# A constant tile of the decoder-trunk kernel declared 24 columns wide, 16 of them used

## The chip, the core and the metric

One core of a Trainium2 chip runs the whole kernel. The metric is the device time of one execution in microseconds (us). The profile is of one execution of the same program; its span runs from the first to the last instruction. The engines are TensorE (PE, with its weight loads listed apart as PEld), VectorE (DVE), ScalarE (ACT), GpSimd (POOL) and the DMA queues, most of them issued from SyncE (SP).

## What is computed

One layer of a hybrid decoder trunk on x of 512 positions by 2048 features, all in float32:

```
h = rms_norm(x, norm1_w)
proj = h @ w_in                       # 2048 x 5648: q, k, v | z, xBC | dt
attn = moba_attention(rms_norm(q), rms_norm(k), v)      # 8 heads of 128, causal blocks of 256
xbc  = silu(causal_dwconv(xBC))       # width 4
dt   = softplus(dt_raw + dt_bias);  a = -exp(a_log)     # 16 heads
y    = ssd_chunked_scan(xs, dt, a, bm, cm) + d_skip * xs
ssm  = rms_norm(y * silu(z))
x = x + concat(attn, ssm) @ w_out     # 2048 x 2048
u = causal_dwconv(rms_norm(x) @ w_up) # 2048 x 11264, width 3
return x + (silu(u_gate) * u_val) @ w_down              # 5632 x 2048
```

The tile that is changed holds exp(a_log), once per partition: 16 float32 values, one per head.

## The kernel before

**Splitting.** Every large product is made of fp32r matmuls. An operand v is split into `hi` = v rounded to fp32r (ACT, lines 1428 and the like) and `lo` = v - hi (DVE, line 1437 and the like), and a product is hi.hi + hi.lo + lo.hi: three matmuls for each pair of 128x128 stationary and 128xN moving tile. Each matmul loads its own stationary tile (LDWEIGHTS) before it streams the moving one. In the profile's names, `x<-cmb,hi` is output, then moving tile, then stationary tile.

**Stages, in order of time.**
1. To 78 us: z and the first quarter of v. The x tiles A (hi) and B (lo), 16 of each, are stationary; the split weights `hi2`/`lo2` move (names `s<-hi,A`, `y<-hi,A`, 512 and 256 columns).
2. 78 to 298 us: q, k of five heads and x, B, C, by 2x2 block products of which only seven are computed instead of eight (P1 to P7), for 11 groups of column blocks. A product is 24 matmuls of 256 columns: `hi2`/`lo2` are stationary. P1, P2 and P3 move A and B; P4, P5, P6 and P7 move the tile TK, which holds sums and differences of blocks of x.
3. 298 to 753 us: the rest of the projection (names `acc<-hi,A` and `acc<-A,hi`), attention (tiles `qh`, `ql`, `kh`, `kl`, `PTh`, `PTl`, `vh`, `vl`), the scan, and the projection w_out with A, B moving in 512 columns.
4. 753 to 2095 us: the main part. 44 groups for w_up, then 24 for w_down (three passes over 7, 8 and 7 blocks), each again seven products; the moving operand is one of the seven tiles cmb0 to cmb6 (hi and lo halves of eight 256-column blocks), the stationary one `hi2`/`lo2`. A w_up product is 24 matmuls (8 x 3), a w_down product 21 or 24. In code, with h, l the split weights and bk the cmb tile:

```
for q in part:
    w = h[:, q * 128:(q + 1) * 128]
    pe.matmul(out, w, bk[:, 0, q, :], ...)          # line 1693
    pe.matmul(out, w, bk[:, 1, q, :], ...)          # line 1694
for q in part:
    pe.matmul(out, l[:, q * 128:(q + 1) * 128], bk[:, 0, q, :], ...)   # line 1696
```

Around each product k of stage 4 a list written out by hand sets the order: the product's output is taken from PSUM (lines 1540 to 1568), then sums of weight blocks for later products (lines 1409 to 1417 on DVE, 1402 on POOL), the `lo` of product k+2 (`split_lo`, line 1437), the convolution and gating work (lines 1578 to 1603), and the `hi` of product k+3 (`split`, line 1428). Weight blocks are loaded six to eight products ahead into `rawa` and `rawb`. There are three `hi2` buffers and two `lo2` buffers.

**Where tiles lie.** On-chip memory is given out from two ends. Pools on the left grow upwards from a low address, in the order in which they are opened, pools on the right downwards from the top, and every tile's row is rounded up to a multiple of 32 bytes. `ea_log` (line 301) is the last tile of the pool `consts`, the first pool on the left. Behind it on the left come `ring` (rawa, hi2, lo2), `ab` (A, B; later `w2`: par2, rawb, acc_s) and `rb` (rawb of stage 2). On the right lie TK, all cmb tiles, the attention and scan tiles and the work tiles of the later stages. Several tiles are used from a column offset on: hi2 and lo2 from column 20, 36 or 52 (`W_OFF`, lines 1427, 1436, 1097, 1104), A and B from 36 (`X_OFF`), TK from 20, cmb from 4 (`F_OFF`).

First byte used, counted along a partition, in the program before (slices within a tile begin multiples of 64 bytes later):

| tile | side | address of first byte used | remainder by 64 | by 256 |
|---|---|---|---|---|
| hi2 / lo2, stages 1 and 3 | left | 23424 / 36480, + 80, buffers 4352 apart | 16 | 208 |
| hi2 / lo2, stage 2 | left | same, + 208 | 16 | 80 |
| hi2 / lo2, stage 4 | left | same, + 144 | 16 | 16 |
| A0..A15, B0..B15 | left | 45184 and 82048, + 144, 2304 apart | 16 | 16 |
| TK | right | 155360 + 80 | 48 | 48 |
| cmb0 to cmb4 / cmb5 / cmb6 | right | 146144, 16640 apart / 112864 / 129504, each + 16 | 48 | 240 |
| PTh, PTl | right | 120640 and 124736, + 512 | 0 | 64 |
| vh, vl | right | 172640, 176736 or 221152, 225248 | 32 | 96 or 224 |
| kl, ql | right | 158144 and 152000, buffers 2048 apart | 0 | 192 |
| qh | right | 164288, buffers 2048 apart | 0 | 192 |
| kh | right | 168544, buffers 2048 apart | 32 | 96 |

ea_log itself is written by one ACT exponential (line 436) and read by one DVE instruction (line 448), both over 16 columns.

Of the kernel before, what the change touches and what calls it, by code (L numbers as in the profile page):

```python
# [20 lines left out]
F32 = mybir.dt.float32  # L21
# [186 lines left out]
def body(ctx, tc, xT, wi, wz, wq, wv1, wv, wz1, wo, wu, wd0, wd1, wd2, pp, pf, outT, dbg={}):  # L208
# [6 lines left out]
    consts = ctx.enter_context(tc.tile_pool(name="consts", bufs=1))  # L215
# [82 lines left out]
    rstd = consts.tile([128, 4], F32, name="rstd")  # L298
    epsms = consts.tile([128, 4], F32, name="epsms")
    nhalf = consts.tile([128, 8], F32, name="nhalf")  # L300
    ea_log = consts.tile([128, 16], F32, name="ea_log")

    def pc(name, i=0, n=1):
        o = _PC[name] + i
# [1426 lines left out]
```

## Time and profile before

| | |
|---|---|
| median of 3 runs | 2097.41 us (2097.01 to 2098.18) |
| the profiled execution | 2097.41 us; its span 2095.7 us |
| mean granted TensorE clock | 0.999 |
| PE busy | 2079.4 us, 99% of the span |
| PEld busy | 2004.7 us, 96% |
| DVE busy | 1646.0 us, 79% |
| ACT busy | 1033.1 us, 49% |
| POOL busy | 229.3 us, 11% |
| DMA | 349.77 MB, 167 GB/s on average |
| stage 4 | 753 to 2095 us |

A matmul's row shows from start to modelled end some 0.28 us for 256 columns, but matmuls are pipelined: what counts is the distance from one start to the next, which is what "pace" means below. It is found by dividing a stretch of time by the number of matmuls that start in it.

### The profile page before, as it was taken

How to read it: one execution, taken by the hardware profiler on the slowest of the kernel's cores; microseconds unless marked ns; L12 is line 12 of the kernel's file. 1: busy time of each engine (PE TensorE's matmuls, PEld its weight loads, DVE VectorE, ACT ScalarE, POOL GpSimd, SP SyncE). 2: the span in 40 equal slices, each digit the busy share in tenths (PEclk: the TensorE clock that was granted, in tenths of full speed). 3: DMA queues.
4: the chain of work that ended last, by engine and by line, in shares of the span. 5: the costliest groups of instructions: out<-in, count | busy, mean ns of one | idle time of the engine just before them, and what ended most of it. 6: DMA issues, size and time to landing. Idle time of an engine off the chain costs nothing.

```text
span 2095.7 us, 39004 instructions
## 1 busy us (share of the span) xinstructions
PE 2079.4 (99%) x15958; PEld 2004.7 (96%) x15958; DVE 1646.0 (79%) x2209; ACT 1033.1 (49%) x1467; POOL 229.3 (11%) x137
## 2 busy tenths in 40 slices
PE   9999999999999999999999999999999999999999
PEld 8999998898888899999999999999999999999998
DVE  7787856656655479889898988988989987866876
ACT  7545444554444345454454544545445645544532
POOL 0011100000100001101011010110101111111110
PEclk9999999999999999999999999999999999999999
DMA  5544443343445454444444544544446668657753
GB/s 173 181 151 153 170 159 127 131 151 126 136 141 181 160 185 160 146 159 156 156 162 142 181 151 142 178 143 163 154 159 220 214 178 244 215 161 230 233 193 112
DMA packets 125778, 349.77 MB, mean 167 GB/s; under 512 B 12000, under 2 KB 36512, under 8 KB 122784
## 3 DMA queue, kind: packets, MB, share of 16 engines
q1 hardware_dynamic: 123296, 338.90, 47.4%
q0 software_dynamic: 2304, 8.39, 2.4%
q8 instruction: 125, 2.05, 0.4%
q14 instruction: 53, 0.43, 0.1%
HBM read 293.20 MB, written 54.03 MB: 166 GB/s over the span
## 4 chain that ended last, share of the span: by engine, by line
PE 97%; DVE 2%; ACT 1%; issue 0%; DMA 0%; SPq 0%; ACTq 0%; DVEq 0%
PE x L1694 18%; PE x L1693 18%; PE x L1696 18%; PE acc L203 16%; PE x L203 9%; PE sm L203 4%; PE y L1694 3%; PE y L1696 3%; PE y L1693 3%; PE y L203 3%; PE s L203 2%; DVE lo L1437 0%; DVE cmb L1488 0%; DMA rawa<-wz 0%; ACT hi L203 0%
## 5 line engine op out<-in xcount | busy, mean ns | idle before, releaser
L1693 PE MATMUL x<-cmb,hi 128*128 128x256 f32 x3152 | 773.6, 282 | 3.6 <-ACT hi L1428 1.9
L1694 PE MATMUL x<-cmb,hi 128*128 128x256 f32 x3152 | 773.8, 283 | 0.0
L1693 PEld LDWEIGHTS x<-cmb,hi 128*128 128x128 f32 x3152 | 592.8, 188 | 5.1 <-issue 3.9
L1694 PEld LDWEIGHTS x<-cmb,hi 128*128 128x128 f32 x3152 | 596.0, 189 | 0.0
L1696 PE MATMUL x<-cmb,lo 128*128 128x256 f32 x3152 | 444.4, 283 | 0.7 <-DVE lo L1437 0.6
L1696 PEld LDWEIGHTS x<-cmb,lo 128*128 128x128 f32 x3152 | 406.4, 189 | 1.4 <-DVE lo L1437 1.4
L1428 ACT ACTIVATE hi<-s 128x1024 fp32r<-128x1024 f32 (+1 forms) x203 | 202.5, 998 | 244.3 <-DVE s L1409 125.8
L1437 DVE TENSOR_TENSOR lo<-s,hi 128x1024 fp32r<-128x1024 f32 (+1 forms) x203 | 241.0, 1187 | 38.8 <-issue 36.2
L1402 POOL TENSOR_TENSOR rawb<-rawa,rawb 128x1024 f32<-128x1024 f32 (+1 forms) x66 | 161.2, 2443 | 928.2 <-DVE s L1409 907.9
L1437 DVE TENSOR_TENSOR lo<-rawa,hi 128x1024 fp32r<-128x1024 f32 (+1 forms) x206 | 244.4, 1186 | 19.7 <-PE x L1696 15.8
L1428 ACT ACTIVATE hi<-rawa 128x1024 fp32r<-128x1024 f32 (+1 forms) x206 | 211.4, 1027 | 16.0 <-PE x L1694 15.5
L203 DVE TENSOR_TENSOR lo<-rawa,hi 128x1024 fp32r<-128x1024 f32 (+3 forms) x119 | 136.0, 1143 | 68.5 <-PE acc L203 36.2
L1560 ACT ACTIVATE cP<-x 128x256 f32<-128x256 f32 x131 | 50.5, 386 | 238.8 <-PE x L1696 238.8
L203 ACT ACTIVATE hi<-rawa 128x1024 fp32r<-128x1024 f32 (+3 forms) x120 | 118.6, 989 | 93.7 <-PE acc L203 71.2
L203 PE MATMUL acc<-A,hi 128*128 128x512 f32 x352 | 139.6, 397 | 0.0
L203 PE MATMUL acc<-A,lo 128*128 128x512 f32 x352 | 136.8, 389 | 0.0
L203 PE MATMUL acc<-B,hi 128*128 128x512 f32 x352 | 136.7, 388 | 0.0
L1694 PE MATMUL y<-cmb,hi 128*128 128x256 f32 x544 | 133.6, 283 | 0.0
L1693 PE MATMUL y<-cmb,hi 128*128 128x256 f32 x544 | 133.4, 282 | 0.0
L1437 DVE TENSOR_TENSOR lo<-rawb,hi 128x1024 fp32r<-128x1024 f32 (+1 forms) x67 | 79.9, 1192 | 39.5 <-PE x L1696 38.2
L1694 PEld LDWEIGHTS y<-cmb,hi 128*128 128x128 f32 x544 | 102.8, 189 | 0.0
L1693 PEld LDWEIGHTS y<-cmb,hi 128*128 128x128 f32 x544 | 102.3, 188 | 0.0
(277 smaller groups left out, 3428.1 us busy)
## 6 DMA issues: line engine op xcount, KB each, us to landing
rawa<-wu SPq DMA_DIRECT2D x176, 512.0 KB, 3.7
rawa<-wd SPq DMA_DIRECT2D x64, 448.0 KB, 4.1
rawa<-wi SPq DMA_DIRECT2D x44, 512.0 KB, 3.9
gd<-gt SPq DMA_DIRECT2D x22, 1024.0 KB, 4.2
rawb<-wu SPq DMA_DIRECT2D x43, 512.0 KB, 4.6
rawa<-wo SPq DMA_DIRECT2D x32, 512.0 KB, 3.7
rawa<-wd SPq DMA_DIRECT2D x32, 512.0 KB, 4.0
ld<-gd SPq DMA_DIRECT2D x27, 512.0 KB, 7.3
```

The costliest lines, as they stand in the source:

```text
L203: return fn(out, *args, **kw)
L1402: (po if gi != 1 else ve).tensor_tensor(r, raw[gi, "11"][:, :n], r, op=OP.subtract)
L1428: se.activation(h[:, :n], src[:, :n], AF.Copy)
L1437: ve.tensor_tensor(l[:, :n], src[:, :n], h[:, :n].bitcast(F32), op=OP.subtract)
L1560: se.activation(g[x], X[:, 256:512] if x == "P5" else X[:, :256], AF.Copy)
L1693: pe.matmul(out, w, bk[:, 0, q, :], start=fresh and q == 0, stop=False, skip_group_check=True)
L1694: pe.matmul(out, w, bk[:, 1, q, :], start=False, stop=False, skip_group_check=True)
L1696: pe.matmul(out, l[:, q * 128:(q + 1) * 128], bk[:, 0, q, :], start=False, stop=q == n - 1, skip_group_check=True)
```

## The change

The tile is declared with 24 columns and cut back to its first 16. Its rounded row grows from 64 to 96 bytes, so the pools behind it on the left (ring, ab, rb, w2) begin 32 bytes later. Tiles of consts, and all tiles on the right, stay where they are. No instruction, size, wait or order is edited.

```
-    ea_log = consts.tile([128, 16], F32, name="ea_log")
+    ea_log = consts.tile([128, 24], F32, name="ea_log")[:, :16]
```

## The prediction, made before the changed kernel was run

> **What bounds the kernel.** I read the page's totals and its chain of waits first, then the costliest groups, then busy times by stage, and then starts of single matmuls.
>
> ```profile
> span 2095.7 us, 39004 instructions
> PE 2079.4 (99%) x15958; PEld 2004.7 (96%) x15958; DVE 1646.0 (79%) x2209; ACT 1033.1 (49%) x1467; POOL 229.3 (11%) x137
> ...
> PE 97%; DVE 2%; ACT 1%; issue 0%; DMA 0%; SPq 0%; ACTq 0%; DVEq 0%
> PE x L1694 18%; PE x L1693 18%; PE x L1696 18%; PE acc L203 16%; PE x L203 9%; PE sm L203 4%; PE y L1694 3%; PE y L1696 3%; PE y L1693 3%; PE y L203 3%; PE s L203 2%; DVE lo L1437 0%; DVE cmb L1488 0%; DMA rawa<-wz 0%; ACT hi L203 0%
> ```
>
> TensorE carries 97% of the chain and hardly ever waits. So the time is the number of matmuls times their pace, and only a change of pace can move it much. The pace in the main part, w_up and w_down, comes from a table by stretches (columns: length, busy time and instructions of each engine, granted clock, DMA share, GB/s) and from the counts of the groups.
>
> ```profile
> 753.00:1641.00 888.00, 887.05 (x7394) 886.85 (x7393) 799.92 (x990) 452.28 (x587) 107.88 (x44) 1.00 0.47 162
> 1641.00:2095.00 454.00, 447.69 (x3710) 445.45 (x3708) 346.05 (x401) 212.42 (x271) 69.52 (x39) 1.00 0.64 200
> ...
> 1000.00:1403.20 403.20, 403.20 (x3362) 403.20 (x3361) 362.47 (x450) 201.25 (x260) 49.14 (x20) 1.00 0.45 157
> ```
> ```profile
> L1693 PE MATMUL x<-cmb,hi 128*128 128x256 f32 x3152 | 773.6, 282 | 3.6 <-ACT hi L1428 1.9
> L1693 PE MATMUL y<-cmb,hi 128*128 128x256 f32 x544 | 133.4, 282 | 0.0
> ```
>
> In 403.20 us 3360 matmuls start (3362 touch the stretch, two of them begun before it): a pace of 120.0 ns at full granted clock. Lines 1693, 1694 and 1696 each have 3152 + 544 = 3696 of them, 11,088 in all, and 11,088 x 120.0 ns = 1330.6 us is nearly all of stage 4.
>
> The row that decides the prediction is in stage 2, where the same three-matmul pattern with 256 columns runs with two kinds of moving tile. Rows of the order of time (start, length, what):
>
> ```profile
> 157.72 0.28 PE L203 MATMUL x<-A,hi 128*128 128x256 f32 x1
> ...
> 159.53 1.07 PE L203 MATMUL x<-A,lo 128*128 128x256 f32 x8
> 160.44 2.08 PE L203 MATMUL x<-TK,hi 128*128 128x256 f32 x16
> 162.35 1.12 PE L203 MATMUL x<-TK,lo 128*128 128x256 f32 x8
> 163.31 0.88 PE L203 MATMUL x<-TK,hi 128*128 128x256 f32 x6
> ```
>
> A product that moves A and B takes 160.44 - 157.72 = 2.72 us for 24 matmuls, a pace of 113.3 ns. The next, which moves TK, takes 163.31 - 160.44 = 2.87 us, a pace of 119.6. Stationary buffers, columns, clock and code are the same. By the table of addresses, A and B lie at 16 past a multiple of 64 bytes, as the stationary hi2 and lo2 do, and TK lies at 48. The cmb tiles of stage 4 also lie at 48 against stationary tiles at 16, and run at TK's pace.
>
> Two more pairs separate readings of this. In attention, PTh and PTl (remainder 0) move against vh and vl (remainder 32), and kl (0) moves against qh (0), with ql (0) loaded next.
>
> ```profile
> 609.98 0.28 PE L203 MATMUL sm<-PTh,vh 128*128 128x256 f32 x1
> ...
> 611.39 0.40 PE L203 MATMUL acc<-A,hi 128*128 128x512 f32 x1
> ```
> ```profile
> L203 PE MATMUL acc<-A,lo 128*128 128x512 f32 x352 | 136.8, 389 | 0.0
> ...
> L203 PE MATMUL sm<-kh,ql 128*128 128x512 f32 x8 | 3.2, 396 | 0.0
> L203 PE MATMUL sm<-kl,qh 128*128 128x512 f32 x8 | 3.1, 389 | 0.0
> ```
>
> The 12 matmuls of PTh and PTl take 611.39 - 609.98 = 1.41 us, a pace of 117.5: slow, although the moving tile begins on a multiple of 64. In 512 columns, kl against qh takes 389 ns from start to end, as A against lo2 does (16 against 16), and kh against ql (32 against 0) 396; that last pair is weak evidence, since another kind of matmul follows it. So neither remainder of the moving tile alone explains the pace. What fits all rows is the difference of the two: no difference modulo 64 is fast (16/16, 0/0), a difference of 32 slow (48/16, 0/32, 32/0). By 256 the fast differences are 0, 64 and 192, the slow ones 96, 160 and 224, moving minus stationary. That the two streams, a matmul's moving tile and the next one's weights, get in each other's way in memory is my reading, not something a row names.
>
> **The change, part by part.** No instruction is added or taken away; ea_log's writer and reader keep address and size, so that part costs nothing, and needs no cover. All else is the shift of the left side by 32 bytes.
>
> *Stage 4.* Stationary hi2/lo2 go from 16 to 48, the cmb tiles stay at 48: difference 0 modulo 64, and 240 - 48 = 192 modulo 256, exactly that of A against hi2 in stage 2 (16 - 80), which ran at 113.3. So 11,088 x (120.0 - 113.3) ns = 74 us less. Bounds: nothing gained at one end; the other end is that row's 113.3, the fastest pace of any 256-column product shown.
>
> *Stage 2.* The products that move TK become 48/48, difference 192 modulo 256 too.
>
> ```profile
> L203 PE MATMUL x<-TK,hi 128*128 128x256 f32 x688 | 89.6, 283 | 1.0 <-DVE u L203 0.6 <-ACT cP L203 0.4
> ...
> L203 PE MATMUL x<-TK,lo 128*128 128x256 f32 x344 | 48.2, 282 | 0.0
> ...
> L203 PE MATMUL y<-TK,hi 128*128 128x256 f32 x16 | 2.1, 282 | 0.0
> ...
> L203 PE MATMUL y<-TK,lo 128*128 128x256 f32 x8 | 1.1, 282 | 0.0
> ```
>
> 688 + 344 + 16 + 8 = 1056 matmuls x (119.6 - 113.3) ns = 7 us less.
>
> *Left against left* (A, B with hi2, lo2, in stages 1 to 3) shifts together and keeps its differences; attention and scan lie on the right and do not move: nothing, between zero and the cost in the second rival.
>
> *Who is late next.* With 168 matmuls of a w_up group at 113.3 ns, PE needs 19.04 us instead of 20.16. DVE is the next engine:
>
> ```profile
> 1378.12:1398.28 20.16, 20.16 (x170) 20.16 (x169) 18.15 (x25) 10.06 (x14) 2.45 (x1) 1.00 0.41 138
> ...
> 1620.16:1640.32 20.16, 20.16 (x170) 20.16 (x169) 19.51 (x23) 14.32 (x19) 2.72 (x1) 1.00 0.44 137
> 1640.32:1660.48 20.16, 19.64 (x162) 19.25 (x161) 20.16 (x24) 14.15 (x19) 2.72 (x1) 1.00 0.74 252
> ...
> 1781.44:1801.60 20.16, 20.07 (x167) 19.90 (x167) 20.16 (x21) 14.57 (x19) 3.82 (x2) 1.00 0.92 296
> ...
> 1942.72:1962.88 20.16, 19.98 (x166) 19.77 (x166) 20.16 (x25) 13.46 (x17) 3.60 (x2) 1.00 0.88 279
> ```
>
> DVE's 362.47 us in the twenty groups from 1000 to 1403.20 are 18.1 us a group, 0.9 below PE's new need, so w_up stays bound by PE. At the three changes of pass, where the splits of the cmb tiles (line 1488) come on top, DVE is already busy all of 20.16 us, and PE cannot run ahead of it: each such stretch keeps its length over one to two groups, 1.1 to 2.2 us not gained, 3 to 7 us together; I take 5. ACT (10.06 of 20.16) and the DMA (share 0.45) have room for loads that come 6% more often.
>
> Sum: 74 + 7 - 5 = 76 us less than 2097.4, which is both the profiled execution's own time (span 2095.7 and 1.7 around it) and the median of the three runs: **2021 us**.
>
> **Rivals.** *No change.* The pace could hang on something that differs between A and TK other than the low bits: A and B step 2304 bytes from one block to the next, TK and cmb 1024. Against it: the stationary tiles step 512 bytes, so the two streams meet at many multiples of 256 apart, and within stage 2 every A product is fast and every TK product slow; and cmb5 (from 112864) overlies addresses of B14 and B15, which are fast in stage 2. For it: no row shows cmb, or any right-hand moving tile of 1024-byte steps, going fast. The time would then be 2097.4. The Trainium skill, page "TensorE: Matmul & The Clock Gate", section "Step-by-step: what each phase is for", says TensorE has two independent read ports and that "Loading the next tile's weights doesn't steal SBUF read bandwidth from the running matmul." By that rule the relative address cannot matter, and the change would give the same 2097.4; the A and TK rows (113.3 against 119.6) speak against it, unless the cause lies elsewhere.
>
> *Slower.* The slow case could be "either tile begins in the upper half of 64 bytes": 48/16, 0/32 and 32/0 fit that as well, and no row shows a pair with both in the upper half. Then stage 4 stays at 120, and what is fast now, at 16/16, turns slow at 48/48.
>
> ```profile
> L203 PE MATMUL acc<-A,hi 128*128 128x512 f32 x352 | 139.6, 397 | 0.0
> ...
> L203 PE MATMUL x<-A,hi 128*128 128x256 f32 x168 | 39.5, 277 | 0.6 <-DVE v L203 0.6
> ...
> L203 PE MATMUL acc<-hi,A 128*128 128x256 f32 x128 | 37.7, 295 | 0.0
> ...
> L203 PE MATMUL acc<-hi,A 128*128 128x512 f32 x64 | 26.2, 410 | 0.0
> ...
> L203 PE MATMUL s<-hi,A 128*128 128x512 f32 x64 | 25.2, 394 | 0.0
> ...
> L203 PE MATMUL y<-A,hi 128*128 128x256 f32 x96 | 22.7, 278 | 0.0
> ...
> L203 PE MATMUL acc<-hi,A 128*128 128x272 f32 x64 | 19.3, 302 | 0.5 <-ACT v L203 0.5
> ...
> L203 PE MATMUL y<-hi,A 128*128 128x256 f32 x64 | 18.1, 282 | 2.6 <-ACT hi L203 2.6
> ```
>
> By three matmuls each (hi.hi, hi.lo, lo.hi) that is 3 x (352 + 64 + 64) = 1440 of 512 columns and 3 x (168 + 128 + 96 + 64 + 64) = 1560 of 256 or 272. At 6.3 ns each for the narrow ones, and for the wide ones from 6.3 (if the cost is one for a matmul) to 12.6 (if it goes by columns), 19 to 28 us more: 2116 to 2125. It decides if A's products in stage 2 go from 2.72 to 2.87 us. Two streams meeting gives no reason for a fixed half, so I hold it less likely.
>
> *DVE takes the bound.* If DVE's 2.0 us of idle time a group (20.16 - 18.1) did not shrink, because its waits for PE and ACT in order cost the same, w_up would gain nothing: stage 4's gain falls to the 24 w_down groups, 3696 x 6.7 ns = 25 us, and with stage 2's 7 and the 5 lost at the pass changes 27 us less, 2070. Half of it gives about 2046. Against it: most of that idle time is waiting for PE itself, and `lo` of a product is issued two products ahead.
>
> **How the numbers follow.** Difference modulo 64, gain nearly whole (2010 to 2045): 0.76. DVE takes half or more (2045 to 2075): 0.08. No change: 0.09. Slower: 0.07. A measurement of this kernel tells about 0.2%, 4 us, from no change; so faster 0.84, same 0.09, slower 0.07. The range runs from 2008, where neither pass changes nor waits take anything back, with the rounding of the paces, to 2060, which takes in most of the third rival and leaves out no change and slower.
>
> **What would show it.** Right: in stage 4 a w_up product's 24 matmuls in 2.72 us instead of 2.88, TK's products likewise, A's unchanged, a group in about 19.0 us, DVE busy over 94% of w_up. Wrong: stage 4 still at 120 ns (rival one), A's products at 2.87 (rival two), or 113 ns within products with waits of PE for `lo` (line 1437) between them (rival three).

## The result, and the profile after

The changed kernel takes 2024.24 us (median of 4 runs, 2024.06 to 2024.38), against 2097.21 us for the kernel before beside it: a ratio of 0.9652, 95% interval 0.9635 to 0.9668, 73.0 us less. The profiled execution took 2024.33 us. Totals and chain of waits of the page after:

```profile
span 2022.6 us, 39004 instructions
...
PE 2002.2 (99%) x15958; PEld 1925.6 (95%) x15958; DVE 1640.7 (81%) x2209; ACT 1034.6 (51%) x1467; POOL 231.0 (11%) x137
...
PE 93%; DVE 4%; DMA 1%; issue 1%; ACT 1%; SPq 0%; DVEq 0%; ACTq 0%
```

The instruction counts are those of before, one for one. PE's busy time falls by 77 us and DVE's by 5: the same matmuls went faster. Busy times by stretches (w_up, w_down, then twenty w_up groups):

```profile
748.00:1589.50 841.50, 839.53 (x7398) 838.67 (x7397) 797.62 (x990) 454.85 (x589) 108.94 (x44) 1.00 0.50 172
1589.50:2022.60 433.10, 423.87 (x3693) 420.37 (x3691) 342.95 (x400) 210.62 (x269) 69.88 (x39) 1.00 0.67 208
...
1000.00:1380.80 380.80, 380.80 (x3363) 380.80 (x3362) 361.36 (x451) 201.68 (x260) 49.63 (x20) 1.00 0.48 167
```

The 3360 matmuls that start in the last stretch now take 380.80 us instead of 403.20: 113.3 ns each instead of 120.0, at the same granted clock of 1.00. In stage 2 (order of time; start, length, what):

```profile
155.32 0.28 PE L203 MATMUL x<-A,hi 128*128 128x256 f32 x1
...
157.13 1.07 PE L203 MATMUL x<-A,lo 128*128 128x256 f32 x8
158.04 1.98 PE L203 MATMUL x<-TK,hi 128*128 128x256 f32 x16
159.85 1.07 PE L203 MATMUL x<-TK,lo 128*128 128x256 f32 x8
160.76 1.98 PE L203 MATMUL x<-TK,hi 128*128 128x256 f32 x16
```

The product that moves A still takes 158.04 - 155.32 = 2.72 us. TK's takes 160.76 - 158.04 = 2.72 too, where it took 2.87.

How much came from where: the first row of each fence below is the first matmul of stage 4, the second the last seven of its last product, before and then after.

```profile
752.85 0.28 PE L1693 MATMUL x<-cmb,hi 128*128 128x256 f32 x1
...
2091.03 1.00 PE L1696 MATMUL x<-cmb,lo 128*128 128x256 f32 x7
```
```profile
746.48 0.28 PE L1693 MATMUL x<-cmb,hi 128*128 128x256 f32 x1
...
2018.01 0.95 PE L1696 MATMUL x<-cmb,lo 128*128 128x256 f32 x7
```

Stage 4 begins 6.4 us earlier, nearly all of it from stage 2 (the matmul that began at 73.9 us begins 0.3 earlier, the one at 314.2 us 6.5 earlier), and gains 73.0 - 6.4 = 66.6 us itself. Its 11,088 matmuls at 113.33 instead of 120.0 ns would give 73.9, so 7.3 were given back. The chain of waits after shows where (start, length, what it went through):

```profile
751.60 2.48 DMA xd<-gx
754.10 6.07 DMA ld<-xd
760.19 1.07 ACT cmb L1522
762.43 1.06 DVE s L1417
763.72 1.14 DVE lo L1437
764.90 1.21 PE x L1696 x8
1569.78 1.13 DVE lo L1437
...
1584.22 1.09 PE x L1696 x7
```

And DVE at the three changes of pass (by stretches, columns as above):

```profile
1584.80:1604.00 19.20, 18.04 (x152) 17.30 (x151) 19.20 (x23) 13.68 (x19) 2.71 (x1) 1.00 0.77 256
1730.00:1745.00 15.00, 13.82 (x117) 13.26 (x116) 15.00 (x16) 10.75 (x13) 4.15 (x2) 1.00 0.86 273
1884.00:1898.00 14.00, 12.87 (x107) 12.13 (x106) 14.00 (x18) 8.24 (x11) 3.59 (x2) 1.00 0.88 265
```

DVE is busy all the time there and PE has gaps of 1.1 to 1.2 us in each. Added up over all distances between starts in stage 4, what lies above the pace is 15.7 us after and 8.5 before. Of the 7.2 more, 5.5 lie at the three changes of pass (2.5, 1.5 and 1.5) and 1.0 in the first 25 us of stage 4, counting only distances more than 60 ns above the pace; smaller distances make up the remaining 0.8. In those 25 us the chain goes through transfers of `xd` and `ld`, which do not get shorter: by the pages' medians 2.6 and 5.9 us before, 2.5 and 6.6 after.

### The profile page after: what moved, and what is told of

Its sections match the earlier page's. It is cut to its first block, busy times and chain, and to the rows that moved or that the text cites. A ratio compares the mean times of both kernels' runs of the same rounds, so it can differ in the third digit from the quotient of the medians.

```text
span 2022.6 us, 39004 instructions
## 1 busy us (share of the span) xinstructions
PE 2002.2 (99%) x15958; PEld 1925.6 (95%) x15958; DVE 1640.7 (81%) x2209; ACT 1034.6 (51%) x1467; POOL 231.0 (11%) x137
## 4 chain that ended last, share of the span: by engine, by line
PE 93%; DVE 4%; DMA 1%; issue 1%; ACT 1%; SPq 0%; DVEq 0%; ACTq 0%
PE acc L203 17%; PE x L1696 17%; PE x L1693 17%; PE x L1694 17%; PE x L203 8%; PE sm L203 5%; PE y L1693 3%; PE y L1694 3%; PE y L1696 3%; PE y L203 3%; PE s L203 2%; DVE lo L1437 1%; DVE cmb L1488 1%; DVE lo L203 0%; DVE s L1417 0%
## 5 line engine op out<-in xcount | busy, mean ns | idle before, releaser
L1693 PE MATMUL x<-cmb,hi 128*128 128x256 f32 x3152 | 736.4, 276 | 6.0 <-ACT hi L1428 3.0
L1694 PE MATMUL x<-cmb,hi 128*128 128x256 f32 x3152 | 734.6, 275 | 0.0
L1696 PE MATMUL x<-cmb,lo 128*128 128x256 f32 x3152 | 424.1, 275 | 1.6 <-DVE lo L1437 1.4
L1696 PEld LDWEIGHTS x<-cmb,lo 128*128 128x128 f32 x3152 | 387.7, 188 | 2.8 <-DVE lo L1437 2.8
L1694 PE MATMUL y<-cmb,hi 128*128 128x256 f32 x544 | 126.7, 275 | 0.0
L1693 PE MATMUL y<-cmb,hi 128*128 128x256 f32 x544 | 126.7, 275 | 0.0
```

The source lines that it names most:

```text
L1693: pe.matmul(out, w, bk[:, 0, q, :], start=fresh and q == 0, stop=False, skip_group_check=True)
L1694: pe.matmul(out, w, bk[:, 1, q, :], start=False, stop=False, skip_group_check=True)
```

## The experiments

Below, "difference" is the first byte of the moving tile minus that of the stationary one, modulo 256, in stage 4. It was 224 in the kernel before and is 192 in the changed one. The theory of the prediction was that the difference modulo 64 sets the pace; the rivals here are a place of the weights alone, or of some other tile on the left. All kernels keep every instruction of before unless it is said.

**Reach the same difference another way.** Three edits to the kernel before, by column offsets (4 bytes a column): the weights of stage 4 alone by 32 bytes; the cmb tiles alone by 32; the change and the cmb tiles together, back to difference 224.

```
e1  before, lines 1427, 1436:  hi_tile(36), lo_tile(36)  ->  hi_tile(44), lo_tile(44)     # 192
e2  before, line 36:           F_OFF = 4  ->  12                                          # 0
e3  changed kernel, line 36:   F_OFF = 4  ->  12                                          # 224
```

> ea_log as before, 16 wide; only the split weights of stage 4 begin 32 bytes later in their tiles, so hi2/lo2 lie at 48 against cmb at 48. Difference theory (the pace hangs on the address of the moving tile minus that of the weights, modulo 64): stage 4 at 113.3 ns, TK's products still at 119.6, so 2024 + 7 = 2031 us. Weights' place (stationary tiles are faster at 48 than at 16, wherever the moving ones lie): 2031 as well. Other left tiles (rawa, rawb, A, B, acc_s or the DMA into them gained from the shift): 2097.

> ea_log 16 wide, weights at 16 as before; the cmb tiles are used from column 12 instead of 4, so they lie at 16 (48 + 32 modulo 64). Difference theory: stage 4 at 113.3, 2031 us. Weights' place: weights unmoved, 2097. Other left tiles: 2097.

> ea_log 24 wide as in the change, and cmb from column 12: weights at 48, cmb at 16, difference 32 again. Difference theory: stage 4 back at 120 ns, only stage 2 gains, 2097 - 7 = 2090 us. Weights' place and other left tiles: both as after the change, 2024.

Measured: e1 2029.77 us (ratio 0.9678, 0.9662 to 0.9694), e2 2081.08 (0.992, 0.9905 to 0.9935), e3 2091.13 (0.997, 0.996 to 0.9981). Twenty w_up groups, 3360 starts, in e1, e2 and e3 in turn:

```profile
1000.00:1380.80 380.80, 380.80 (x3363) 380.80 (x3362) 361.34 (x451) 201.91 (x260) 49.44 (x20) 1.00 0.48 167
```
```profile
1000.00:1397.60 397.60, 397.60 (x3363) 397.60 (x3362) 362.43 (x451) 201.58 (x261) 49.26 (x20) 1.00 0.46 159
```
```profile
1000.00:1403.20 403.20, 403.20 (x3363) 403.20 (x3362) 362.50 (x451) 201.42 (x260) 49.12 (x20) 1.00 0.45 157
```

The paces are 113.3, 118.3 and 120.0 ns. e1 shows that the weights of stage 4 are all that matters of the left side there, and leaves 2029.77 - 2024.24 = 5.5 us for stage 2. e3 has every left tile where the change puts it, and is slow again: neither the weights' place alone nor another left tile is the cause, the places of weights and moving tile together are. But e2 refutes modulo 64: there the two begin on the same remainder by 64, and the pace is 118.3.

**How far does it go?** ea_log declared 32 columns wide (left side 64 bytes later than before), and then, from the changed kernel, other columns for the weights of stage 4.

```
e4     before, line 301:               [128, 16]  ->  [128, 32] cut to [:, :16]    # 160
m64    changed, lines 1427 and 1436:   column 36  ->  4                            # 64
m128                                   36  ->  52                                  # 128
m176                                   36  ->  40                                  # 176
m208                                   36  ->  32                                  # 208
m32                                    36  ->  12                                  # 32
m96                                    36  ->  60                                  # 96
```

> ea_log declared 32 wide: the left side shifts by 64 bytes instead of 32. Difference theory, period 64: every difference modulo 64 as before, 2097 us. If the period is 128 or 256 the differences are new (cmb minus weights 160 instead of 224 modulo 256) and the time may be anything between 2024 and 2097. Other left tiles: some of the gain stays, well below 2097.

> The changed kernel with the weights of stage 4 taken from column 4 instead of 36, 128 bytes earlier: moving minus stationary goes from 192 to 64 modulo 256, nothing else. So far (256-column pace in stage 4): 0: 118.3, 160: 116.7, 192: 113.3, 224: 120.0 ns. Period 128: 64 is the same as 192, 113.3 ns, 2024 us. Period 256: 64 is a place of its own, anything from 109 to 120 ns, 2024 - 48 = 1976 to 2024 + 74 = 2098 us; another pace than 113.3 refutes period 128.

> The changed kernel with the weights of stage 4 taken from column 52: difference 128 modulo 256. Period 128: as difference 0 (118.3 ns), 2024 + 11088 x 5.0 ns = 2079 us. Period 256: another pace. If the cost were a matter of how far apart the two streams are within the period, a half period from 0 would be the fastest, at or below 113.3 ns, 2024 us or less.

> The changed kernel with the weights of stage 4 taken from column 40: difference 176 modulo 256, 16 bytes from the fast 192 towards the 160 that ran at 116.7 ns. If the cost goes by pieces of 32 bytes, 176 is as 160 (116.7 ns, 2024 + 11088 x 3.4 ns = 2062 us) or as 192 (113.3 ns, 2024 us). If it goes smoothly with the difference, half way: 115.0 ns, 2043 us.

> The changed kernel with the weights of stage 4 taken from column 32: difference 208 modulo 256, 16 bytes from the fast 192 towards the slow 224. By pieces of 32 bytes: as 192 (113.3 ns, 2024 us) or as 224 (120.0 ns, 2024 + 74 = 2098 us). Smoothly: half way, 116.7 ns, 2061 us.

> The changed kernel with the weights of stage 4 taken from column 12: difference 32 modulo 256. The multiples of 32 tried so far gave 0: 118.3, 64: 118.3, 128: 120.0, 160: 116.7, 192: 113.3, 224: 120.0 ns. If only a narrow place near 192 is fast: 116.7 to 120 ns, 2024 + 11088 x (3.4 to 6.7) ns = 2062 to 2098 us. If every second or third place were as fast as 192 and the change did not need just this one: 113.3 ns, 2024 us.

> The changed kernel with the weights of stage 4 taken from column 60: difference 96 modulo 256, the last multiple of 32 not tried. Narrow place near 192: 116.7 to 120 ns, 2062 to 2098 us. Otherwise 113.3 ns, 2024 us.

The same twenty groups in e4, m64, m128, m176, m208, m32 and m96 in turn:

```profile
1000.00:1392.00 392.00, 392.00 (x3362) 392.00 (x3361) 362.44 (x451) 201.67 (x261) 49.33 (x21) 1.00 0.47 162
```
```profile
1000.00:1397.60 397.60, 397.60 (x3362) 397.60 (x3361) 362.32 (x452) 201.63 (x260) 49.36 (x20) 1.00 0.45 160
```
```profile
1000.00:1403.20 403.20, 403.20 (x3362) 403.20 (x3361) 362.50 (x450) 201.39 (x261) 49.12 (x20) 1.00 0.45 157
```
```profile
1000.00:1400.80 400.80, 400.80 (x3363) 400.80 (x3362) 362.41 (x451) 201.41 (x260) 49.22 (x20) 1.00 0.45 158
```
```profile
1000.00:1400.40 400.40, 400.40 (x3362) 400.40 (x3361) 362.37 (x451) 201.36 (x260) 49.13 (x20) 1.00 0.45 158
...
1830.00:1900.00 70.00, 70.00 (x603) 70.00 (x602) 45.29 (x45) 30.29 (x40) 10.70 (x7) 1.00 0.66 196
```
```profile
1000.00:1397.60 397.60, 397.60 (x3363) 397.60 (x3362) 362.52 (x451) 201.46 (x261) 49.18 (x21) 1.00 0.45 160
```
```profile
1000.00:1403.20 403.20, 403.20 (x3362) 403.20 (x3361) 362.51 (x450) 201.29 (x260) 49.12 (x20) 1.00 0.45 157
```

| difference | kernel | pace, ns | time, us |
|---|---|---|---|
| 0 | e2 | 118.3 | 2081.08 |
| 32 | m32 | 118.3 | 2075.07 |
| 64 | m64 | 118.3 | 2074.16 |
| 96 | m96 | 120.0 | 2091.47 |
| 128 | m128 | 120.0 | 2092.07 |
| 160 | e4 | 116.7 | 2062.05 |
| 176 | m176 | 119.3 | 2084.17 |
| 192 | changed kernel; e1 | 113.3 | 2024.24; 2029.77 |
| 208 | m208 | 119.2 | 2081.71 |
| 224 | before; e3 | 120.0 | 2097.21; 2091.13 |

(e1 and e2 lack stage 2's gain, as before does.) Of ten places, eight of them all the multiples of 32, only 192 is fast; 16 bytes to either side it is 119. A period of 64 is out (0 and 128 against 192), and so is one of 128 (64 against 192). The seven cmb tiles lie on both remainders by 512, and within w_up the products of all seven have the same pace in each kernel (to 0.1 ns), so 256 is enough as a period. That the difference alone sets the pace was tried with more than one pair of places at 192 and 224 only: 192 is 113.3 with cmb at 240 against weights at 48, A at 16 against 80, and TK at 48 against 112 (all modulo 256); 224 is 119.6 to 120.0 with cmb at 240 against 16, cmb at 16 against 48, and TK at 48 against 80. Every other row of the table stands for one pair of places. Neither smoothness nor steps of 32 bytes held: 176 is slower than both its neighbours. In m208 the pace also depends on more than the difference, since the last quoted row of it, in the pass with eight blocks, has 600 starts in 70.00 us, 116.7 ns, against 119.2 in w_up. No formula for the pace came out of this map.

**Which weights does a moving tile meet: its own, or the next one's?** The kernel before with only `lo2` moved to difference 192 (line 1436), `hi2` left at 224; and the kernel before with half as many stationary columns in lines 1694 and 1696.

```
lo_only  line 1436:  lo_tile(36)  ->  lo_tile(44)
half_w   line 1694:  pe.matmul(out, w, ...)        ->  pe.matmul(out[:64, :], w[:, :64], ...)
         line 1696:  pe.matmul(out, l[.. 128], ..) ->  pe.matmul(out[:64, :], l[.. 64], ..)
```

> The kernel before (ea_log 16 columns) with only lo2 of stage 4 taken 32 bytes later: hi2 stays at difference 224 from cmb, lo2 goes to 192. If each matmul's pace goes with its own pair or with the weights loaded beside it, the third of the matmuls that uses lo2 runs at 113.3 and the rest at 120: mean 117.8 ns, 2097.7 - 3696 x 6.7 ns = 2073 us, and starts in a run of lo2 matmuls 113 to 114 ns apart. If the pace is one rhythm of the whole stream, set by its slower part, 120 throughout: 2098 us.

> The kernel before, with 64 instead of 128 stationary columns in the matmuls of lines 1694 and 1696, so hi.lo and lo.hi are added to the first 64 output partitions only; the number of matmuls, their 256 moving columns and all addresses stay (difference 224). Two streams meeting: the 16 of 24 matmuls beside which a half load runs lose much of the 6.7 ns: pace 113.3 to 117, 2097.7 - 11088 x (3 to 6.7) ns = 2023 to 2064 us. If the load of the weights has no part in it and the moving stream alone is slow: 120 ns, 2098 us.

Measured: lo_only 2074.91 us (0.9888, 0.9872 to 0.9904), half_w 2075.92 (0.9895, 0.9879 to 0.9911). Both have 3360 starts in 395.80 us, 117.8 ns:

```profile
1000.00:1395.80 395.80, 395.80 (x3363) 395.80 (x3362) 362.43 (x451) 201.46 (x261) 49.25 (x20) 1.00 0.46 160
```
```profile
1000.00:1395.80 395.80, 395.80 (x3362) 395.80 (x3362) 362.44 (x451) 201.18 (x260) 49.31 (x20) 1.00 0.46 160
```

Starts in lo_only, in order of time:

```profile
1001.42 1.07 PE L1696 MATMUL y<-cmb,lo 128*128 128x256 f32 x8
1002.33 0.28 PE L1693 MATMUL x<-cmb,hi 128*128 128x256 f32 x1
...
1004.25 1.07 PE L1696 MATMUL x<-cmb,lo 128*128 128x256 f32 x8
```

The eight `lo` matmuls take 1002.33 - 1001.42 = 0.91 us, some 114 ns each; the sixteen `hi` ones 1.92 us, 120.0 each. So the pace belongs to single matmuls, not to one rhythm of the stream, and the price is as expected. The ends of these runs tell which. Over the products after 800 us, a `lo` matmul followed by `lo` is followed after 113 ns (median). The last `lo`, beside which the next `hi2` is loaded, is followed after 117; the last `hi`, beside which `lo2` is loaded, after 114. In the kernel before both are 124, in the changed one 114 and 113. (Within a slow product the distances are not equal: in the kernel before their medians go 118, 117, 122, 124 over and over, so 117 is one of the slow ones, and 120 is their mean.) A matmul's own stationary tile would give the opposite. What counts is the moving tile and the weights loaded while it moves. That agrees with the reading in the prediction. It speaks against the rule of the Trainium skill cited there, page "TensorE: Matmul & The Clock Gate", section "Step-by-step: what each phase is for", that loading the next tile's weights takes no SBUF read bandwidth from the running matmul: here a matmul beside such a load takes up to 6.7 ns more than the 113.3 of the fastest place, by where the two lie. Whether bandwidth is what is short, no run shows.

half_w fits neither expectation. Starts in it:

```profile
1001.14 1.08 PE L1696 MATMUL x<-cmb,lo 128*64 128x256 f32 x8
1002.07 0.28 PE L1693 MATMUL y<-cmb,hi 128*128 128x256 f32 x1
1002.18 0.28 PE L1694 MATMUL y<-cmb,hi 128*64 128x256 f32 x1
1002.30 0.28 PE L1693 MATMUL y<-cmb,hi 128*128 128x256 f32 x1
...
1003.97 1.08 PE L1696 MATMUL y<-cmb,lo 128*64 128x256 f32 x8
```

In the `lo` run, where all loads but the last are halves, eight take 0.93 us, 116 ns each. The sixteen `hi` ones, half of whose loads are halves, take 1003.97 - 1002.07 = 1.90 us, 119 each, and gain nearly nothing; over the whole trace the distance beside a half load is even the longer one there, 123 ns (median) against 117 beside a full load. So in the `lo` run half loads go with a shorter pace, with the moving data and its address unchanged, but the gain is not in proportion to the columns loaded. These matmuls also write 64 output partitions instead of 128, and this run does not tell the two apart. How the two streams collide stays open.

## Why the prediction was right

*What bounds it.* Right: with PE busy 99% of the span before and after, a pace shorter by 6.7 of 120.0 ns in stage 4 (and for TK) came out as a time shorter by 73 of 2097 us.

*Stage 4's term,* 74 us: right in place and size. The pace is the 113.3 ns that was read off A in stage 2, and 73.9 us is what it is worth.

*Stage 2's term,* 7 us: 6.4 by the start of stage 4, 5.5 by e1 against the changed kernel.

*The sum* was 76 and 73.0 were measured. The mis-sized term is what comes back: 5 was taken, from a range of 3 to 7, and 7.3 was measured. The changes of pass themselves account for 5.5 of it, close to the 5 taken; what the sum had left out is the start of stage 4 (1.0) and smaller distances along the way (the rest). PE's waits on the splits, before and then after:

```profile
PE x L1693 <- ACT hi L1428: 1.9, 3, 1.0
...
PE x L1696 <- DVE lo L1437: 0.6, 2, 0.4
```
```profile
PE x L1693 <- ACT hi L1428: 3.0, 6, 1.1
...
PE x L1696 <- DVE lo L1437: 1.4, 4, 0.5
```

*The law,* "no difference modulo 64 is fast", was wrong, and the number did not rest on it alone. Its evidence for 0 and 64 as fast came from 512-column rows by their lengths from start to modelled end (389 ns for kl against qh and for A against `lo2`), and at 256 columns both run at 118.3. From start to start, the 512-column matmuls that move A and B at difference 64 are 226 to 227 ns apart (medians, kernel before), and those at 192 are 225 (`s<-hi,A`) and 231 (`s<-lo,A`): the map found at 256 columns does not carry over to 512. What carried the prediction is the sentence that 192 modulo 256 was "exactly that of A against hi2 in stage 2": a row with the same shape, stationary buffers and difference. By the law alone e2, m64 and m128 would have been at 2024 to 2031 us with the changed kernel; they took 2074 to 2092. That a step of 32 bytes led to 192 and not to one of these is, as far as the law goes, luck; as far as that row goes, it is not. The same change with 32 columns instead of 24 gives 2062.

*Rivals.* No change is refuted by the result. Slower by halves of 64 bytes is refuted by A's unchanged 2.72 us. DVE as the bound is not seen: in w_up it is busy 797.62 of 841.50 us, 95%, and from 770 to 1584 us no distance between starts is more than 60 ns above the pace; PE's longer waits lie at the start of stage 4, at the changes of pass and at the end.

## What to carry to other kernels

When the same matmul pattern of 256 columns runs at two paces at one granted clock, compare the addresses of the moving tile and of the weights loaded beside it, modulo 256, and copy the difference of a fast row exactly; a rule guessed from a few rows is less safe than a row. A pad of 32 bytes in an unrelated tile can move a whole pool, and the next 32 bytes can take back half of what it brought (e4: 2062), or nearly all, if they move the other operand (e3: 2091), so the pace is to be read again after any change of layout. Where one wants the difference and not the accident, offset the operand itself, as e1 does.

## What was not expected of the hardware

In a stream in which each 256-column matmul loads its own 128 stationary columns, the pace goes from 113.3 to 120.0 ns with the difference of two addresses, in a pattern that is not smooth: of ten differences modulo 256 one is fast (192) and its neighbours 16 bytes away, at 119.3 and 119.2, are nearly as slow as any. The cost follows the weights loaded next, not those in use, and halving the stationary columns of two in three matmuls at difference 224 took the time from 2098.21 to 2075.92 us, against 2029.77 with full loads at 192 (e1).
